# A hybrid block in float32: its gates in blocks of 1024 columns, 14 of 48 groups of eight products as seven, heads from the value projections on, x loaded a second time

## The chip, the cores and the metric

The kernel runs on one core of one Trainium2 chip. Each engine works through its own queue in order: PE (matmuls, with PEld for its weight loads), DVE (VectorE), ACT (ScalarE), POOL (GpSimd) and SP, which here issues most of the DMAs. Times are device microseconds of one execution. The metric is the median of several runs; a separate, profiled execution gives the trace.

## The reference

One transformer block in float32, 256 tokens, width 2048.

```python
h = rms_norm(x, g_mix)
fq, fk, fv, f_logit, sq, sk, sv, mq, gates = split(h @ w_in)
# six forgetting heads, six stick-breaking heads, four memory heads of 128
g = sigmoid(gates.reshape(b, s, 3, 2048) + b_gate)
merged = g[:, :, 0] * (o_fox @ w_br_fox) + g[:, :, 1] * (o_sb @ w_br_sb) + g[:, :, 2] * (o_mem @ w_br_mem)
x = x + merged @ w_out
u = causal_depthwise_conv(rms_norm(x, g_ffn) @ w_up, conv_w, conv_b)
u_gate, u_val = split(u)
x = x + (silu(u_gate) * u_val) @ w_down
```

The gates are the largest product before the feed-forward part: 256 x 2048 times 2048 x 6144.

## The kernel before, in words

**Products.** Every weight is used as a high part, rounded to the matmul's operand type, and a low part, the rest. A product of a 128 x 128 tile of the left side with 128 x 512 weights is three matmuls into one PSUM bank: high times high, low times high, high times low (`passes`, L153). `product` (L161) walks the 2048 rows of a 512-column stripe of weights in pieces of two k tiles. A piece (`piece`, L140) is a DMA of 512 KB on SP into `raw`, a cast on ACT to `hi` (L146) and a subtraction on DVE to `lo` (L147); four buffers of each are in rotation. For two k tiles, two row tiles t of x and one stripe a piece feeds 12 matmuls.

**Order.** `product` calls `tick()` (L110) after each piece. Generators that were put on a list with `later` move on by one stage at each tick, two of them at a time: this is how the attention heads run between the pieces of a projection. `finish()` runs those that are left. A scheduler may move instructions that aren't held in program order (`pin`, L134, holds them while `pinned[0]` is set; `tc.keep_in_program_order` always does).

**Stages around the change.** Projections for the heads come first: names `f0` to `f4` for the forgetting heads, `s0` to `s4` for the stick-breaking ones, where `s3` and `s4` are the values (L595 to L602). The six stick-breaking heads (`sb_head`, L614) are put on the list behind `s4`; each has a product of scores (tile `z`), three functions on ACT, sums along the keys by matmul (tile `r`), an exponential, and the weighted values. Then for each of four 512-column stripes n: three gates (L664 to L673), each with its own `product`, its bias row `bg`, and a read-out on DVE (L670) that scales by the row's norm and adds the bias, with a sigmoid on ACT; then the three branch products, multiplied by the gates (L680 to L687) and transposed. The output projection adds to `xres`, which has held x since the start (L716), and the sum is stored (`xkeep`, L717).

**Eight and seven.** The down projection at the end works in blocks of 1024 columns. There a group is two k tiles, two row tiles and two stripes: eight products, or seven in a scheme that multiplies sums and differences of tiles (`seven`, L966). Four factors are made from the left side (`forms`, L879), four sums from the weights: `T1` to `T4`. In that stage two of these sums are made ahead and come ready from memory (L980), two are made on the spot (L982, L983). `Y` are four further banks that collect products used in more than one place; `gather` (L1014) adds them where they belong.

Of the kernel before, what the change touches and what calls it, by code (L numbers as in the profile page):

```python
# [37 lines left out]
PLANS = ("eeeee" + "se" * 5 + "sse" + "s" + "eee", "e" + "se" * 3 + "sse" * 4 + "see")  # L38
AHEAD = 2
NSEVEN = tuple(plan.count("s") for plan in PLANS)  # L40


@with_exitstack
def hybrid_block(
# [83 lines left out]
    def finish():  # L128
        while waiting or active:
            tick()  # L130
# [458 lines left out]
    for c in range(3):  # L589
# [4 lines left out]
        later(heads_T(y, qs[c], gs, 0, f"s{c}"))  # L594
    ps = proj(C_SB + 1536, 512, "s3")  # L595
    vs[0] = rows_of(block("vs0"))
    for t in range(NT):
        nc.scalar.activation(vs[0][:, t], ps[t], AF.Copy, scale=rstd[:, t : t + 1])
    ps = proj(C_SB + 2048, 256, "s4")
    vs[1] = rows_of(block("vs1"))  # L600
    for t in range(NT):
        nc.scalar.activation(vs[1][:, t, :256], ps[t][:, :256], AF.Copy, scale=rstd[:, t : t + 1])  # L602

    W3 = 3 * P
# [9 lines left out]
    def sb_head(h):  # L614
# [21 lines left out]
        diagonal(lb)  # L636
        yield 2
        weighted(lb, vs, h, N_FOX + h, Z)

    for h in range(N_SB):  # L640
        later(sb_head(h))


# [16 lines left out]

    for n in range(4):
        n0 = n * 512
        gate = []
        for b in range(3):  # L664
            bg = gp.tile([P, 512], F32, tag="bg", name=f"bg_{n}_{b}")
            tc.keep_in_program_order(nc.sync.dma_start(bg, b_gate[0, b, n0 : n0 + 512].partition_broadcast(P)))
            ps = proj(C_GATE + b * D + n0, 512, f"g{n}_{b}")
            g = rows_of(block(f"g_{n}_{b}"))
            for t in range(NT):
                nc.vector.scalar_tensor_tensor(g[:, t], ps[t], rstd[:, t : t + 1], bg, ALU.mult, ALU.add)  # L670
            if n > 0:
                nc.scalar.activation(g, g, AF.Sigmoid)
            gate.append(g)  # L673
        if n == 0:
            finish()
            for g in gate:
                nc.scalar.activation(g, g, AF.Sigmoid)
        acc = rows_of(block(f"acc_{n}"))
        for i, (w, k0, nk, b) in enumerate(branches):
            ps = product(lambda k: oT[:, k0 + k], w[0], nk, n0, 512, f"b{n}_{b}")  # L680
            for t in range(NT):
                g = gate[b]
                if i == 0:
                    nc.vector.tensor_tensor(acc[:, t], g[:, t], ps[t], ALU.mult)
                else:
                    nc.vector.tensor_tensor(g[:, t], g[:, t], ps[t], ALU.mult)
                    nc.vector.tensor_tensor(acc[:, t], acc[:, t], g[:, t], ALU.add)  # L687
        later(merged_T(acc, n))
# [4 lines left out]
    rbc = cst.tile([P, S], F32, name="rbc")  # L693

# [43 lines left out]
    def conv_pool():  # L738
        assert not waiting and not active
        xrs.close()  # L740
# [395 lines left out]
```

## Time and profile before

| | |
|---|---|
| median of 3 runs | 1488.44 us (1487.39 to 1489.52) |
| the profiled execution | 1488.21 us |
| its span, first to last instruction | 1486.5 us |
| PE busy | 1479.5 us, 7408 matmuls |
| DVE busy | 1047.6 us |
| ACT busy | 860.4 us |
| gates (group g of PE, lines L157 to L159) | 3 x 384 = 1152 matmuls of 128 x 512 |
| PE clock granted | 1.000 |

A row of a group names line, engine, operation, out <- in, shapes, count, busy time, mean duration in ns, idle time of the engine just before and what ended it. A matmul's end is modelled, so durations on PE overlap; the distance of starts is the pace. A window's row gives start and end, its length, then busy time and instructions of PE, PEld, DVE, ACT and POOL, the clock, the DMA share and GB/s. A row of waits gives who waited for whom, the total, how often, and the longest.

### The profile page before, as it was taken

The page shows a single profiled execution, that of the slowest core. Times are in us where ns is not written, and L with a number is a line of the kernel's source. Part 1 is how long each engine was busy: PE and PEld are TensorE (multiplying, and loading weights), DVE is VectorE, ACT ScalarE, POOL GpSimd, SP SyncE. Part 2 cuts the span into 40 slices and gives each one's busy share as a digit, 9 for nine tenths or more (in the row PEclk, how much of TensorE's full clock was granted, in tenths as well). Part 3 has the DMA queues.
Part 4 walks back from the last instruction along what each step waited for, and adds up shares of the span by engine and source line. Part 5 has one row for each costly group of instructions (what it writes and reads, how often), then busy time and mean ns, then how long its engine had stood idle before and what let it go on. Part 6 is the DMA issues. An engine that isn't in the chain of part 4 may idle for free.

```text
span 1486.5 us, 20239 instructions
## 1 busy us (share of the span) xinstructions
PE 1479.5 (100%) x7408; PEld 1248.4 (84%) x7408; DVE 1047.6 (70%) x1353; ACT 860.4 (58%) x1231; POOL 40.9 (3%) x91
## 2 busy tenths in 40 slices
PE   9999999999999999999999999999999999999998
PEld 7888888888888888888888888888888888888887
DVE  5767566554655656556556877877877886999997
ACT  6755454358544444444456776776676676665664
POOL 1000000001000000000000000000000000000000
PEclk9999999999999999999999999999999999999999
DMA  8675475475676666656677778778778787777874
GB/s 294 190 203 156 128 223 160 121 228 155 187 203 204 192 203 202 201 187 208 199 222 223 236 268 269 239 267 281 231 274 274 236 275 235 247 252 267 282 284 170
DMA packets 156804, 329.80 MB, mean 222 GB/s; under 512 B 11456, under 2 KB 19952, under 8 KB 156704
## 3 DMA queue, kind: packets, MB, share of 16 engines
q1 hardware_dynamic: 151216, 311.52, 66.6%
q0 software_dynamic: 4736, 15.93, 2.9%
q8 instruction: 58, 0.95, 0.3%
q10 hardware_dynamic: 752, 1.06, 0.2%
q14 instruction: 42, 0.34, 0.1%
HBM read 313.78 MB, written 14.68 MB: 221 GB/s over the span
## 4 chain that ended last, share of the span: by engine, by line
PE 96%; ACT 1%; DVE 1%; DMA 1%; issue 1%; POOL 0%; SPq 0%; DVEq 0%; POOLq 0%; ACTq 0%
PE u L838 22%; PE u L840 11%; PE g L157 5%; PE g L159 5%; PE g L158 5%; PE d L926 5%; PE d L927 5%; PE d L925 5%; PE s L157 2%; PE s L159 2%; PE f L157 2%; PE f L159 2%; PE f L158 2%; PE s L158 2%; PE b L157 2%; PE b L159 2%
## 5 line engine op out<-in xcount | busy, mean ns | idle before, releaser
L838 PE MATMUL u<-hT,hi_u 128*128 128x512 f32 x1408 | 442.4, 396 | 0.1
L840 PEld LDWEIGHTS u<-hT,lo_u 128*128 128x128 f32 x1408 | 264.4, 188 | 62.6 <-DVE lo_u L147 0.2
L840 PE MATMUL u<-hT,lo_u 128*128 128x256 f32 x1408 | 276.7, 278 | 0.0
L147 DVE TENSOR_TENSOR lo_u<-raw_u,hi_u 128x1024 fp32r<-128x1024 f32 x176 | 211.9, 1220 | 81.1 <-ACT hi_u L146 78.8
L146 ACT CAST hi_u<-raw_u 128x1024 fp32r<-128x1024 f32 x176 | 180.5, 1048 | 116.3 <-DMA raw_u<-in_w_up_dram 70.3
L838 PEld LDWEIGHTS u<-hT,hi_u 128*128 128x128 f32 x1408 | 214.3, 189 | 0.5 <-issue 0.5
L147 DVE TENSOR_TENSOR lo_g<-raw_g,hi_g 128x1024 fp32r<-128x1024 f32 x96 | 117.7, 1228 | 101.2 <-ACT hi_g L146 98.5
L146 ACT CAST hi_g<-raw_g 128x1024 fp32r<-128x1024 f32 x96 | 100.8, 1052 | 121.8 <-PE g L158 98.6
L157 PE MATMUL g<-hi_g,xT 128*128 128x512 f32 x384 | 150.9, 393 | 0.0
L159 PE MATMUL g<-lo_g,xT 128*128 128x512 f32 x384 | 149.6, 390 | 0.0
L158 PE MATMUL g<-hi_g,xT 128*128 128x512 f32 x384 | 149.5, 389 | 0.0
L159 PEld LDWEIGHTS g<-lo_g,xT 128*128 128x128 f32 x384 | 72.1, 188 | 15.3
L158 PEld LDWEIGHTS g<-hi_g,xT 128*128 128x128 f32 x384 | 72.1, 188 | 14.6
L157 PEld LDWEIGHTS g<-hi_g,xT 128*128 128x128 f32 x384 | 72.1, 188 | 14.5
L768 ACT ACTIVATE z<-u,taps 128x256 f32<-128x256 f32 x176 | 74.8, 496 | 0.0
L925 PE MATMUL d<-hi_d,aT 128*128 128x512 f32 x192 | 74.7, 389 | 0.0
L926 PE MATMUL d<-hi_d,aT 128*128 128x512 f32 x192 | 74.7, 389 | 0.0
L927 PE MATMUL d<-lo_d,aT 128*128 128x512 f32 x192 | 74.7, 389 | 0.0
L769 DVE TENSOR_TENSOR y<-y,z 128x512 f32<-128x512 f32 x88 | 60.7, 690 | 19.9 <-ACT z L768 16.4
L147 DVE TENSOR_TENSOR lo_s<-raw_s,hi_s 128x1024 fp32r<-128x1024 f32 (+1 forms) x40 | 44.7, 1118 | 37.2 <-ACT hi_s L146 37.0
L147 DVE TENSOR_TENSOR lo_f<-raw_f,hi_f 128x1024 fp32r<-128x1024 f32 (+1 forms) x40 | 44.7, 1119 | 34.5 <-ACT hi_f L146 33.0
L146 ACT CAST hi_f<-raw_f 128x1024 fp32r<-128x1024 f32 (+1 forms) x40 | 38.6, 967 | 52.5 <-PE f L158 47.6
(333 smaller groups left out, 2817.5 us busy)
## 6 DMA issues: line engine op xcount, KB each, us to landing
raw_u<-in_w_up_dram SPq DMA_DIRECT2D x176, 512.0 KB, 4.7
raw_g<-in_w_in_dram SPq DMA_DIRECT2D x96, 512.0 KB, 3.7
raw_d<-in_w_down_dram SPq DMA_DIRECT2D x48, 512.0 KB, 5.2
r<-in_w_down_dram SPq DMA_DIRECT2D x80, 256.0 KB, 6.5
raw_s<-in_w_down_dram SPq DMA_DIRECT2D x40, 512.0 KB, 5.3
raw_f<-in_w_in_dram SPq DMA_DIRECT2D x32, 512.0 KB, 3.7
raw_s<-in_w_in_dram SPq DMA_DIRECT2D x32, 512.0 KB, 3.6
raw_o<-in_w_out_dram SPq DMA_DIRECT2D x32, 512.0 KB, 4.3
```

Source lines behind the costliest of these rows:

```text
L146: pin(nc.scalar.copy(hi[:, :m], raw[:, :m]))
L147: pin(nc.vector.tensor_tensor(lo[:, :m], raw[:, :m], hi[:, :m].bitcast(F32), ALU.subtract))
L157: nc.tensor.matmul(o, lhsT=xh, rhs=wh, start=first, stop=False)
L158: nc.tensor.matmul(o, lhsT=xl, rhs=wh, start=False, stop=False)
L159: nc.tensor.matmul(o, lhsT=xh, rhs=wl, start=False, stop=last)
L768: nc.scalar.activation(z[:, i], u[:, i, j : j + S], AF.Copy, scale=taps_of(j, i))
L769: nc.vector.tensor_tensor(y, y, z, ALU.add)
L838: nc.tensor.matmul(ps, lhsT=hi[:, j, c], rhs=hT[:, k + j, :], start=first, stop=False)
L840: nc.tensor.matmul(ps[:, :S], lhsT=lo[:, j, c], rhs=hT[:, k + j, :S], start=False, stop=last)
L925: nc.tensor.matmul(o, lhsT=ah, rhs=w[0], start=first, stop=False)
L926: nc.tensor.matmul(o, lhsT=al, rhs=w[0], start=False, stop=False)
L927: nc.tensor.matmul(o, lhsT=ah, rhs=w[1], start=False, stop=last)
```

## The change

The gates are computed in two rounds (nn) of three blocks (b), each of 1024 columns and 2048 rows, in steps. A letter of a plan is a group of two k tiles: `e` has eight products in two steps, `s` seven in four steps. Each step has a preparation (load, cast, subtraction) and a use (matmuls); the preparation runs two steps ahead (`AHEAD`). The sums of weights are made in place over the two loaded pieces, by four adds of 512 columns on DVE. The factors made from x (`xf`) serve all blocks; three pairs of k tiles have them. A block's four banks X are read out after the first step of the block that follows, where the read-out isn't `alone`; the four banks Y by `gather` in three ticks behind the last seven. From the second block of the first round on, casts, subtractions and read-outs are held in program order (`first_pin`), until the round ends.

The stick-breaking heads are on the list before `s3` and `s4`, and each waits for its values by name (`until`). Room for four more raw buffers comes from `xres`: x is given up after its norm and transposes, and loaded again on POOL's queue (`xagain`) behind the second round of gates.

```diff
+GATE_PLANS = (("e" * 8, "esesesee", "esesesee"), ("eeesesee", "esesesee", "esesesee"))
+GATE_SEVENS = 3
...
-    gp = mix.enter_context(tc.tile_pool(name="gp", bufs=3))
+    gp = mix.enter_context(tc.tile_pool(name="gp", bufs=4))
...
         yield 2
+        yield from until(f"vs{h // 4}")
         weighted(lb, vs, h, N_FOX + h, Z)
 
     for h in range(N_SB):
         later(sb_head(h))
-
+    ps = proj(C_SB + 1536, 512, "s3")
...
+    issued.add("vs1")
...
+    xrs.close()
+    gx = ctx.enter_context(ExitStack())
+    gxp = gx.enter_context(tc.tile_pool(name="gx", bufs=1, side="right", reuse_waits="tile"))
...
+    def x_forms(p):
...
+        tt(d, two, v[:, 0, :, 1].unsqueeze(1).to_broadcast([P, 2, 2, P]), ALU.subtract)
+        tt(g, v[:, :, 0, 0], v[:, :, 1, 0], ALU.add)
+        tt(r[:, :2], d[:, :, 0], d[:, :, 1], ALU.add)
+        nc.vector.scalar_tensor_tensor(r[:, FS2], r[:, FS1], -1.0, g[:, 0], ALU.mult, ALU.subtract)
+        tt(r[:, FS4], r[:, FS2], g[:, 1], ALU.add)
+        yield
+        nc.scalar.copy(xf[p][:, :, 0], r)
+        yield
+        tt(xf[p][:, :, 1], r, xf[p][:, :, 0].bitcast(F32), ALU.subtract)
...
+    def load_1k(src, name):
+        turns[0] += 1
+        if turns[0] % 2 == 0:
+            raw = gxp.tile([P, PIECE], F32, tag="more", bufs=4, name=name)
+        else:
+            raw = wp.tile([P, PIECE], F32, tag="raw", name=name)
+        keep(nc.sync.dma_start(raw, src))
+        return raw
...
+    def by_seven(p, src, X, Y, name, first, last):
+        k0, k1 = 2 * p, 2 * p + 1
+        w, raw = {}, {}
+        add = lambda o, i: keep(nc.vector.tensor_tensor(o, o, i, ALU.add))
+
+        def p0():
+            raw[0] = load_1k(src(k0), f"raw_{name}_{k0}")
+            (w["00"],) = halves(raw[0][:, :512], f"{name}_{k0}")
+
+        def p1():
+            raw[1] = load_1k(src(k1), f"raw_{name}_{k1}")
+            w["10"], w["11"] = halves(raw[1], f"{name}_{k1}")
+            add(raw[0][:, :512], raw[0][:, 512:])
+            add(raw[0][:, 512:], raw[1][:, 512:])
+            add(raw[1][:, 512:], raw[0][:, :512])
+            add(raw[1][:, :512], raw[1][:, 512:])
+
+        def p2():
+            w["T1"], w["T3"] = halves(raw[0], f"{name}_{p}t13")
+
+        def p3():
+            w["T4"], w["T2"] = halves(raw[1], f"{name}_{p}t42")
+
+        def u0():
...
+            triple(Y[0], x_of(k0, 0), w["00"], first, last)
+
+        def u1():
+            triple(X[0], x_of(k1, 0), w["10"])
+            triple(X[1], xf_of(p, FS4), w["11"])
+
+        def u2():
+            triple(Y[2], xf_of(p, FS1), w["T1"], first, last)
+            triple(Y[3], xf_of(p, FS3), w["T3"], first, last)
+
+        def u3():
+            triple(Y[1], xf_of(p, FS2), w["T2"], first, last)
+            triple(X[2], x_of(k1, 1), w["T4"])
...
+        def gather():
+            gs.extend(rows_of(block(f"{name}_{n}")) for n in range(2))
...
+            pin(nc.scalar.copy(e, Y[0]))
+            stt(gs[0][:, 0], Y[0], rs(0), bgs[0], ALU.add)
+            tt(e, e, Y[1])
+            yield
+            tt(f, e, Y[2])
+            tt(e, e, Y[3])
+            stt(gs[1][:, 0], f, nr(0), bgs[1], ALU.add)
+            yield
+            stt(gs[0][:, 1], e, rs(1), bgs[0], ALU.add)
+            tt(e, e, Y[2])
+            stt(gs[1][:, 1], e, nr(1), bgs[1], ALU.add)
+
+        def evict():
...
+            for t in range(NT):
+                for n in range(2):
+                    stt(gs[n][:, t], X[2 * t + n], rs(t), gs[n][:, t] if ns else bgs[n], ALU.add)
...
+        end = len(g_steps) - 1
+        behind(end, finish)
+        behind(end if alone else end + 1, evict)
+        for n in range(2):
+            behind(end if alone else end + 5 + n, lambda n=n: curve(n))
...
+    for nn in range(2):
         for b in range(3):
...
+            gate_block(nn, b, GATE_PLANS[nn][b], b == 2)
...
+        if nn == 1:
+            gx.close()
...
+            for n in range(4):
+                c = slice(n * 512, (n + 1) * 512)
+                nc.gpsimd.dma_start(xres[:, :, c], xv[:, :, c])
```

**PE, the second seven of block b = 1 of the first round.** In a name such as `hi_g_1_3`, 1 is the gate and 3 the k tile; `1t` are sums of the seven with number 1; `g_1_x` and `g_1_y` are banks. Before, where a bank is named by gate and row tile (`g_1_0`), the two row tiles of the same k tile in a piece of 512 columns:

```order
L157 MATMUL g_1_0_3075<-hi_g_1_2_3118,xT 128x512
L158 MATMUL g_1_0_3075<-hi_g_1_2_3118,xT 128x512
L159 MATMUL g_1_0_3075<-lo_g_1_2_3119,xT 128x512
L157 MATMUL g_1_1_3076<-hi_g_1_2_3118,xT 128x512
L158 MATMUL g_1_1_3076<-hi_g_1_2_3118,xT 128x512
L159 MATMUL g_1_1_3076<-lo_g_1_2_3119,xT 128x512
```

and in the change:

```order
L715 MATMUL g_1_y_3417<-hi_g_1_2_3462,xT 128x512
L716 MATMUL g_1_y_3417<-hi_g_1_2_3462,xT 128x512
L717 MATMUL g_1_y_3417<-lo_g_1_2_3463,xT 128x512
L715 MATMUL g_1_x_3365<-hi_g_1_3_3480,xT 128x512
L716 MATMUL g_1_x_3365<-hi_g_1_3_3480,xT 128x512
L717 MATMUL g_1_x_3365<-lo_g_1_3_3481,xT 128x512
L715 MATMUL g_1_x_3366<-hi_g_1_3_3480,xf_2922 128x512
L716 MATMUL g_1_x_3366<-hi_g_1_3_3480,xf_2922 128x512
L717 MATMUL g_1_x_3366<-lo_g_1_3_3481,xf_2922 128x512
L715 MATMUL g_1_y_3419<-hi_g_1_1t_3500,xf_2922 128x512
L716 MATMUL g_1_y_3419<-hi_g_1_1t_3500,xf_2922 128x512
L715 MATMUL g_1_y_3420<-hi_g_1_1t_3500,xf_2922 128x512
```

The same weights now feed banks x and y, with x or a factor of it (`xf`) as the left side; a seven has 21 such rows where two k tiles by two stripes had 24.

**DVE, from the read-out of the first block to the first seven of the second.** Before, at the same gate, subtractions follow each other, with heads between:

```order
L147 TENSOR_TENSOR lo_g_0_8_2976<-raw_g_0_8_2974,hi_g_0_8_2975 128x1024
L626 SCALAR_TENSOR_TENSOR sb_2898<-z_2899,sb_2898 128x384
L627 TENSOR_TENSOR sb_2898<-sb_2898,z_2899 128x384
L626 SCALAR_TENSOR_TENSOR sb_2909<-z_2910,sb_2909 128x384
L627 TENSOR_TENSOR sb_2909<-sb_2909,z_2910 128x384
L147 TENSOR_TENSOR lo_g_0_10_3010<-raw_g_0_10_3008,hi_g_0_10_3009 128x1024
```

and in the change:

```order
L809 SCALAR_TENSOR_TENSOR g_0_0_3381<-g_0_x_2944,rstd,bg_g_0_0_2984 128x512
L809 SCALAR_TENSOR_TENSOR g_0_1_3382<-g_0_x_2945,rstd,bg_g_0_1_2986 128x512
L711 TENSOR_TENSOR lo_g_1_1_3390<-raw_g_1_1_3387,hi_g_1_1_3389 128x1024
L756 TENSOR_TENSOR raw_g_1_0_3359<-raw_g_1_0_3359 128x512
L756 TENSOR_TENSOR raw_g_1_0_3359<-raw_g_1_0_3359,raw_g_1_1_3387 128x512
L756 TENSOR_TENSOR raw_g_1_1_3387<-raw_g_1_1_3387,raw_g_1_0_3359 128x512
L756 TENSOR_TENSOR raw_g_1_1_3387<-raw_g_1_1_3387 128x512
L711 TENSOR_TENSOR lo_g_1_0t_3414<-raw_g_1_0_3359,hi_g_1_0t_3413 128x1024
L711 TENSOR_TENSOR lo_g_1_0t_3425<-raw_g_1_1_3387,hi_g_1_0t_3424 128x1024
```

The read-out (L809) stands ahead of the second load's subtraction, and the four adds (L756) between that and the subtractions of the sums.

**ACT, at the scores of a pair of heads.** `sb` is a head's tile; ACT takes Abs, Exp and Ln of its scores z. Before, at the second pair:

```order
L677 ACTIVATE g_0_3070<-g_0_3070 128x1024
L178 CAST oT<-z_2910 128x256
L146 CAST hi_g_1_8_3172<-raw_g_1_8_3171 128x1024
L623 ACTIVATE sb_3095<-z_3096 128x384
L624 ACT_TABLE_LOAD
L624 ACTIVATE sb_3095<-sb_3095 128x384
L623 ACTIVATE sb_3106<-z_3107 128x384
L625 ACT_TABLE_LOAD
L625 ACTIVATE sb_3095<-sb_3095 128x384
```

and in the change:

```order
L710 CAST hi_g_0_11_3030<-raw_g_0_11_3028 128x1024
L616 ACTIVATE sb_2988<-z_2989 128x384
L617 ACTIVATE sb_2988<-sb_2988 128x384
L616 ACTIVATE sb_2999<-z_3000 128x384
L618 ACTIVATE sb_2988<-sb_2988 128x384
L617 ACTIVATE sb_2999<-sb_2999 128x384
L618 ACTIVATE sb_2999<-sb_2999 128x384
```

The gate's sigmoid (L677) no longer comes before a pair, and no table load stands within one. The order of ACT holds 17 table loads before and 5 in the change.

More of the change, by code (lines that the diff above doesn't have):

```diff
@@ L594, in hybrid_block @@
         later(heads_T(y, qs[c], gs, 0, f"s{c}"))
[L595 to L602, printed above, removed]
     W3 = 3 * P
@@ L641, in hybrid_block @@
         later(sb_head(h))
+    ps = proj(C_SB + 1536, 512, "s3")
+    vs[0] = rows_of(block("vs0"))
+    for t in range(NT):
+        nc.scalar.activation(vs[0][:, t], ps[t], AF.Copy, scale=rstd[:, t : t + 1])
+    ps = proj(C_SB + 2048, 256, "s4")
+    issued.add("vs0")
+    vs[1] = rows_of(block("vs1"))
+    for t in range(NT):
+        nc.scalar.activation(vs[1][:, t, :256], ps[t][:, :256], AF.Copy, scale=rstd[:, t : t + 1])
+    issued.add("vs1")
     mT = [None] * (KT // 2)
@@ L659, in merged_T @@
             yield
-    for n in range(4):
-        n0 = n * 512
-        gate = []
-        for b in range(3):
[L665 to L688, printed above, removed]
```

134 lines of the change are left out of this document (132 added, 2 removed).

## The prediction

> **What bounds the kernel now.** I read the page's first part, then the waits of PE, then PE's timeline in the gate stage.
>
> ```profile
> span 1486.5 us, 20239 instructions
> PE 1479.5 (100%) x7408; PEld 1248.4 (84%) x7408; DVE 1047.6 (70%) x1353; ACT 860.4 (58%) x1231; POOL 40.9 (3%) x91
> ```
>
> ```profile
> PE spare L101 <- DVE qscale L251: 1.2, 1, 1.2
> PE kv L159 <- DVE lo_kv L147: 0.5, 1, 0.5
> PE d L926 <- DVE aT L901: 0.3, 1, 0.3
> PE mT L186 <- DMA memres<-in_mem_dram: 0.2, 1, 0.2
> ```
>
> PE is busy for all but 7 us of the span, and no row of its waits lies in the gate stage. So PE's instructions set the end there, and the question is what one of them is worth. The timeline of PE in the gates (start, duration) shows it:
>
> ```profile
> 439.98 0.39 PE L158 MATMUL g<-hi_g,xT 128*128 128x512 f32 x1
> ...
> 474.89 0.39 PE L159 MATMUL g<-lo_g,xT 128*128 128x512 f32 x1
> ```
>
> Between these two stand 154 starts (155 rows, no other PE work): 34.91 / 154 = 0.2267 us from start to start. The 0.39 us that a row shows as its duration runs on under the next one. A matmul taken away is worth 0.227 us, not 0.39; with 0.39 the same sum comes out 1.7 times too large.
>
> **Matmuls removed.** A group of eight products is 8 x 3 = 24 matmuls, 5.44 us; one of seven is 21, 4.76 us. The order of PE has 42 rows fewer, 14 x 3, and after the gates the same rows as before. 42 x 0.2267 = 9.5 us leave the engine that sets the end.
>
> The Trainium skill ("TensorE: Matmul & The Clock Gate", Back-to-back issue gap) gives a stream of loads of weights and matmuls of 512 columns about 131 ns each, and about 216 ns where matmuls stand alone; by these the sum would be, as estimates, 5.5 or 9.1 us. The stream in these rows has a weight load for each matmul and takes 227 ns, so the measurement decides.
>
> **What the sevens ask of DVE and ACT.** The pieces' casts and subtractions, the gates' read-out, the down stage's sums of two halves (the nearest rows for the adds over the loads) and DVE's timeline there:
>
> ```profile
> L147 DVE TENSOR_TENSOR lo_g<-raw_g,hi_g 128x1024 fp32r<-128x1024 f32 x96 | 117.7, 1228 | 101.2 <-ACT hi_g L146 98.5 <-PE r L633 1.5
> L146 ACT CAST hi_g<-raw_g 128x1024 fp32r<-128x1024 f32 x96 | 100.8, 1052 | 121.8 <-PE g L158 98.6 <-PE b L158 20.0 <-DMA raw_g<-in_w_in_dram 1.6
> L670 DVE SCALAR_TENSOR_TENSOR g<-g,rstd,bg 128x512 f32<-128x512 f32 x24 | 17.4, 748 | 0.0
> ```
>
> ```profile
> L921 DVE TENSOR_TENSOR lo_s<-raw_s,hi_s 128x512 fp32r<-128x512 f32 x20 | 13.7, 685 | 0.5 <-ACT hi_s L920 0.5
> L982 DVE TENSOR_TENSOR t<-raw_s 128x512 f32<-128x512 f32 x20 | 13.7, 684 | 0.0
> L983 DVE TENSOR_TENSOR t<-raw_s,raw_s 128x512 f32<-128x512 f32 x20 | 13.7, 684 | 0.0
> ```
>
> ```profile
> 1364.87 0.69 DVE L1028 TENSOR_TENSOR xr<-xr,e 128x512 f32<-128x512 f32 x1
> 1365.59 0.69 DVE L1029 TENSOR_TENSOR e<-e,d 128x512 f32<-128x512 f32 x1
> ...
> 1382.97 1.22 DVE L921 TENSOR_TENSOR lo_s<-raw_s,hi_s 128x1024 fp32r<-128x1024 f32 x1
> 1384.10 0.68 DVE L982 TENSOR_TENSOR t<-raw_s 128x512 f32<-128x512 f32 x1
> 1384.71 0.68 DVE L983 TENSOR_TENSOR t<-raw_s,raw_s 128x512 f32<-128x512 f32 x1
> ```
>
> From start to start a 1024-wide subtraction takes 1.13 us, a half 0.61, and one that reads what the one ahead wrote 0.72. A seven has a half subtraction, three whole ones and four adds, one of which depends on its neighbour: 0.6 + 3.4 + 2.5 = 6.5 us, against 4.76 us of PE. An eight has two subtractions, 2.26 us, against 5.44. A block with three sevens and five eights also reads out eight banks in twelve operations of about 0.7 us, 8.4. That makes 19.5 + 11.3 + 8.4 = 39.2 us of DVE beside 3 x 4.76 + 5 x 5.44 = 41.5 us of PE, 94%. By whole durations it is 3 x 7.1 + 5 x 2.45 + 8 x 0.748 + 4 x 0.684 = 42.3 us, 102%. I take the former, since it is how these rows stand in time, and because the down stage has run so:
>
> ```profile
> 1366.00:1482.00 116.00, 116.00 (x513) 95.87 (x511) 106.61 (x139) 65.36 (x76) 4.34 (x8) 1.00 0.71 249
> 408.00:475.00 67.00, 67.00 (x301) 55.45 (x300) 36.78 (x38) 28.68 (x30) 0.00 (x0) 1.00 0.68 202
> ```
>
> The windows (PE, PEld, DVE, ACT, POOL) give the down stage's second half, with twelve sevens: DVE busy 106.6 of 116 us, 92%, PE 116 of 116. The gates of before (second row) use 55% of DVE. So the gates become what the down stage is already.
>
> The share hides the order, so I walk one "seven, eight" period on the four hi/lo buffers, PE's start of the seven at 0, with a cast 1.05. PE takes the seven's four steps until 0.68, 2.04, 3.40, 4.76, the eight's two until 7.48 and 10.20. A buffer comes free four steps on, so the next seven's casts may start at 3.4, 4.8, 7.5 and 10.2. Its first subtraction ends at 4.8, the second (cast until 5.9) at 7.1, its adds run to 9.6, two of them done at 8.3. The cast of the first pair of sums ends at 9.4, its subtraction at 10.7; the second pair's cast at 11.3, subtraction at 12.4. PE wants them at 12.2 and 13.6. The following eight's cast and subtraction end at 12.4 and 13.5, wanted at 15.0. Slack is 1.2 us or more everywhere: no cost in the steady state, bounds 0 and what the third rival gives.
>
> At a boundary the read-out comes on top. Walked the same way from a block with sevens into the next one, DVE does the gather and two subtractions until 14.9 us after the last seven's start, waits 0.8 for a buffer that PE holds to the block's end, then evicts (2.8) ahead of the next seven's second subtraction; its first sums are ready within 0.3 us of when PE wants them, before or after. Three boundaries are of this kind: 1.0 us, bounds 0 and 5 (the second rival).
>
> The factors made from x are 18 DVE operations of 128 to 512 columns, some 8 us, three casts, in the first block, where eight eights take 18 of 43.5 us of DVE and four heads some 8: hidden. Without that cover they would cost their 8 us once.
>
> **Heads.** Their instructions are the same; they move ahead of two value projections. In the order of ACT the sigmoids no longer stand between heads, and table loads fall from 17 to 5. Before, in the groups of ACT and PE of the stretch that holds the last heads:
>
> ```profile
> L624 ACT ACT_TABLE_LOAD x4 | 5.1, 1283 | 0.1
> L625 ACT ACT_TABLE_LOAD x4 | 5.1, 1283 | 0.1
> L677 ACT ACT_TABLE_LOAD x3 | 3.8, 1283 | 0.1
> L635 ACT ACT_TABLE_LOAD x2 | 2.6, 1283 | 0.0
> L632 PE MATMUL r<-sb,ones 128*128 128x128 f32 x8 | 1.7, 300 | 0.3
> ```
>
> PE waited 0.3 us for a head's sums, behind loads that now go: -0.3. Against it, the steps of the 256-column projection are short, so the first pair has less cover. PE would wait there if the chain still held three or four of those loads, 4 to 5 us once. I take nothing, since the order has none there.
>
> **Loads.** A piece of gate weights is still 512 KB, and eight raw buffers stand in for four.
>
> ```profile
> SPq L145 <- DVE lo_g L147: 204.4, 88, 6.8
> raw_g<-in_w_in_dram SPq DMA_DIRECT2D x96, 512.0 KB, 3.7
> T<-r POOLq DMA_DIRECT2D x20, 512.0 KB, 8.8
> ```
>
> SP's queue waits for buffers, not for landings (204 us in the gates); ACT's row above waited 1.6 us for gate data in 96 casts. 1 MB in 4.76 us is 220 GB/s, under the 249 of the down window. The four reloads of x go out on POOL's queue, which holds nothing else until x is stored; at 8.8 us each, one after another, they take 35 us, and x is first wanted after two branch rounds and one output round, 3 x 96 x 0.2267 = 65 us. Hidden by these; if not, 35 us at most.
>
> **Sum.** The profiled execution took 1488.21 us, 1.7 of them outside the span, and stands 0.2 under the median of the runs. 1488.2 - 9.5 - 0.3 + 1.0 = 1479.4, or 1479.6 beside the median.
>
> **Rivals.**
>
> PE's count decides, as above: 1479.6, chance 0.72.
>
> DVE becomes the bound in the four blocks with three sevens. If its operations take their whole durations, each block is 0.8 us longer than PE's, 3.2, and the boundaries 1.0 to 2.0 more: 5 us, which gives 1483.6. For it: 94 to 102% by the two counts. Against it: the down window. Chance 0.13.
> The Trainium skill ("VectorE: DVE Perf Modes", The DRAIN you can't avoid) says that the next operation starts only when the pipe is empty, with operations that are not held as the exception; by the first half this rival would be the rule. The starts 0.61 us apart of operations of 0.68 are the exception.
>
> The sums' chain sets the pace (the other side). Unlike in the down stage, no part of the sums comes ready from memory: both pairs wait for adds on the two loads. If cast, subtraction, adds and the casts of the sums ran end to end, with the eight's two subtractions ahead, it would be 2.45 + 1.05 + 1.22 + 2.74 + 2 x (1.05 + 1.22) = 12.0 us from the buffer's release at 4.8 to 16.8, where PE wants its eight at 15.0. That is 1.8 us in each of 14 sevens, 25 us: 1503.6. It decides from 0.7 us a seven, where the 9.5 are used up. For it: in-order queues, and ACT behind PE in 98.6 us of waits. Against it: two or more of these run beside each other in the walk. Chance 0.07.
>
> Heads wait in the short projection: 4 us, 1483.6. Chance 0.05. That the matmuls stay is excluded by the order. Mixtures of small waits, 5 to 8 us, hold the last 0.03.
>
> **Numbers.** The low end is the sum without any wait, 1478.6, less 1 us of spread of the runs: 1477.5. The high end takes in the second and fourth case with the same spread: 1485.0. About 0.2%, 3 us, is what a measurement of this kernel can tell from no change. Faster by more: 0.72 + 0.11 + 0.03 = 0.86, since parts of the second and fourth case lie nearer. Slower: 0.07. Within: 0.07.
>
> **What would show it.** In the changed profile: gate matmuls (group g of PE) 1110 instead of 1152 and still 0.227 us apart; PE's waits in the gates under 2 us in all; DVE near 94% in blocks with three sevens; one table load for the sigmoids; x landed well before the first output tile is added. Wrong it is if PE waits for hi or lo of the sums in most sevens (third rival), or if PE's starts stretch over whole blocks while DVE never idles (second).

## The result and the profile after

The changed kernel took 1480.16 us (median of 4 runs, 1478.54 to 1481.43) beside 1488.30 for the kernel before: a ratio of 0.9944, 95% interval 0.9927 to 0.9961. A second set, the same kernel timed among the experiments, gave 1479.75 (5 runs) and 0.9950, 0.9937 to 0.9962. Forecast were 1479.6.

The page of the profiled execution, which took 1481.43 us and was the slowest of its four:

```profile
span 1479.7 us, 20357 instructions
PE 1471.5 (99%) x7366; PEld 1239.8 (84%) x7366; DVE 1134.7 (77%) x1496; ACT 866.9 (59%) x1255; POOL 42.3 (3%) x95
```

42 matmuls fewer (7366 against 7408), and 143 DVE instructions more. PE's timeline tells where the stages begin; first before, then after (start, duration; group `s` are the projections of the stick-breaking heads, `u` the up-projection, `d` the down projection):

```profile
193.61 0.40 PE L157 MATMUL s<-hi_s,xT 128*128 128x512 f32 x1
...
763.99 0.47 PE L838 MATMUL u<-hT,hi_u 128*128 128x512 f32 x1
```

```profile
194.04 0.40 PE L159 MATMUL s<-hi_s,xT 128*128 128x512 f32 x1
...
755.30 0.47 PE L1059 MATMUL u<-hT,hi_u 128*128 128x512 f32 x1
...
1248.76 0.40 PE L1146 MATMUL d<-hi_d,aT 128*128 128x512 f32 x1
```

From `s` to `u` it was 570.38 us and is 561.26: 9.1 us won. Everything that was changed lies between these two. The up-projection behind it, whose code is the same, took 493.46 us here, and 491.68 before: 1.8 us were lost again in this one execution. The table below gives both lengths for each kernel that was run, since the time alone mixes them. (The expectations call the first of them "from the first short projection to the up-projection".)

**PE's pace.** In the second round of gates PE never stops. The first and last of 485 rows in a row that hold one matmul each, all of the gates:

```profile
509.87 0.39 PE L716 MATMUL g_x<-hi_g,xT 128*128 128x512 f32 x1
...
619.59 0.39 PE L717 MATMUL g_x<-lo_g,xT 128*128 128x512 f32 x1
```

109.72 / 484 = 0.2267 us, as before, through two blocks and a half with eight sevens. The first round has seven clearly longer distances of starts: four in the second seven of the second block (1.06 us in excess of the pace), one in the first seven of the third block (0.10) and two in its second seven (0.27). With the small ones, the 366 gate matmuls of these two blocks take 84.45 us from the first start to the last, 1.6 us more than in the kernel without adds below (82.87), which has no long step. The first place:

```profile
382.21 0.39 PE L717 MATMUL g_x<-lo_g,xf 128*128 128x512 f32 x1
382.87 0.50 PE L715 MATMUL g_y<-hi_g_1t,xf 128*128 128x512 f32 x1 [0.26 <-ACT hi_g_1t L710]
...
383.67 0.40 PE L716 MATMUL g_y<-hi_g_1t,xf 128*128 128x512 f32 x1
384.31 0.50 PE L715 MATMUL g_y<-hi_g_1t,xf 128*128 128x512 f32 x1 [0.25 <-ACT hi_g_1t L710]
```

Mind the brackets: they say 0.26 and 0.25 us, since a row's idle time is counted from the modelled end of the matmul ahead. Against the pace of 0.227 the two steps lost 0.43 and 0.41, and the matmul behind each another 0.1. PE waits for the cast of the sums `hi_g_1t`. ACT's timeline shows why it is late:

```profile
373.36 1.28 ACT L844 ACT_TABLE_LOAD   x1
374.65 1.06 ACT L844 ACTIVATE g<-g 128x1024 f32<-128x1024 f32 x1
375.62 1.03 ACT L710 CAST hi_g<-raw_g 128x1024 fp32r<-128x1024 f32 x1
376.56 1.05 ACT L844 ACTIVATE g<-g 128x1024 f32<-128x1024 f32 x1
377.51 1.55 ACT L710 CAST hi_g<-raw_g 128x512 fp32r<-128x512 f32 x2
381.76 1.05 ACT L710 CAST hi_g_1t<-raw_g 128x1024 fp32r<-128x1024 f32 x1 [2.70 <-DVE raw_g L756]
```

The table load and two sigmoids of the block that was just read out, 3.4 us, stand ahead of the casts of the second seven's pieces (377.51); DVE's subtractions and adds follow those, and the cast of the sums waits for the adds (L756).

### The profile page after: what moved, and what is told of

Its sections match the earlier page's. It is cut to its first block, busy times and chain, and to the rows that moved or that the text cites. A ratio compares the mean times of both kernels' runs of the same rounds, so it can differ in the third digit from the quotient of the medians.

```text
span 1479.7 us, 20357 instructions
## 1 busy us (share of the span) xinstructions
PE 1471.5 (99%) x7366; PEld 1239.8 (84%) x7366; DVE 1134.7 (77%) x1496; ACT 866.9 (59%) x1255; POOL 42.3 (3%) x95
## 3 DMA queue, kind: packets, MB, share of 16 engines
q10 hardware_dynamic: 752, 1.06, 0.2%
## 4 chain that ended last, share of the span: by engine, by line
PE 94%; DMA 2%; DVE 2%; ACT 1%; issue 1%; SPq 0%; DVEq 0%; ACTq 0%
PE u L1059 20%; PE u L1061 10%; PE d L1147 5%; PE d L1148 5%; PE d L1146 5%; PE g_x L715 5%; PE g_x L717 5%; PE g_x L716 5%; PE s L159 2%; PE s L161 2%; PE f L161 2%; PE f L159 2%; PE f L160 2%; PE s L160 2%; PE b L161 2%; PE b L159 2%
## 5 line engine op out<-in xcount | busy, mean ns | idle before, releaser
L711 DVE TENSOR_TENSOR lo_g<-raw_g,hi_g 128x1024 fp32r<-128x1024 f32 (+1 forms) x96 | 108.1, 1143 | 34.1 <-ACT hi_g L710 31.7
L710 ACT CAST hi_g<-raw_g 128x1024 fp32r<-128x1024 f32 (+1 forms) x96 | 92.6, 985 | 60.7 <-PE g_x L716 50.4
L715 PE MATMUL g_x<-hi_g,xT 128*128 128x512 f32 x286 | 112.2, 392 | 0.0
L717 PE MATMUL g_x<-lo_g,xT 128*128 128x512 f32 x286 | 111.4, 390 | 0.0
L716 PE MATMUL g_x<-hi_g,xT 128*128 128x512 f32 x286 | 111.3, 389 | 0.0
L149 DVE TENSOR_TENSOR lo_o<-raw_o,hi_o 128x1024 fp32r<-128x1024 f32 x32 | 39.2, 1225 | 35.4 <-ACT hi_o L148 30.9
L148 ACT CAST hi_s<-raw_s 128x1024 fp32r<-128x1024 f32 (+1 forms) x40 | 38.4, 960 | 42.8 <-PE s L160 35.4
L717 PEld LDWEIGHTS g_x<-lo_g,xT 128*128 128x128 f32 x286 | 53.7, 188 | 11.5
```

Of the source, the lines that this page charges most:

```text
L148: pin(nc.scalar.copy(hi[:, :m], raw[:, :m]))
L149: pin(nc.vector.tensor_tensor(lo[:, :m], raw[:, :m], hi[:, :m].bitcast(F32), ALU.subtract))
L710: pin(nc.scalar.copy(hi[:, :n], src))
L711: pin(nc.vector.tensor_tensor(lo[:, :n], src, hi[:, :n].bitcast(F32), ALU.subtract))
L715: nc.tensor.matmul(o, lhsT=a[0], rhs=w[0], start=first, stop=False)
L716: nc.tensor.matmul(o, lhsT=a[1], rhs=w[0], start=False, stop=False)
```

## What the experiments were to tell apart

The theory after the first trace: PE's count makes the gain, the sigmoids cost 1.3 us of it. Rivals: the gain comes from the other parts of the change (blocks, order, heads); DVE has no room left; the sevens slow the up-projection. From the traces, in us (the gaps are what all steps between matmuls of the gates took over PE's pace in the last two blocks of the first round and in the second round, less the 0.1 us that an unbroken stretch of them has in every kernel; the expectations count the long steps alone, 1.3 us in the change):

| kernel | `s` to `u` | gaps | up-projection | median |
|---|---|---|---|---|
| before | 570.38 | 0 | 491.68 | 1488.30 |
| the change | 561.26 | 1.6 | 493.46 | 1480.16 |
| the change again | 561.29 | 1.6 | 496.72 | 1479.75 |
| no sevens | 569.20 | 0 | 491.64 | 1486.84 |
| late sigmoids | 560.73 | 1.1 | 492.74 | 1480.09 |
| split sigmoids, early table | 564.38 | 4.5 | 493.29 | 1481.52 |
| no adds | 559.67 | 0 | 496.68 | 1482.07 |
| late sigmoids, read-out in halves | 559.83 | 0.2 | 496.71 | 1482.57 |
| the same and a 15th seven | 559.75 | 0.6 | 492.43 | 1477.63 |
| two more adds | 565.47 | 5.0 | 491.55 | 1485.19 |
| four sevens a block | 572.05 | 15.4 | 492.64 | 1492.08 |
| heads behind the values | 570.15 | 3.5 | 493.35 | 1488.76 |
| four raw buffers | 582.89 | 23.4 | 491.56 | 1498.00 |
| no rows beside the up-projection | 561.24 | 1.6 | 491.66 | 1479.60 |

## The sevens against the rest of the change

```diff
-GATE_PLANS = (("e" * 8, "esesesee", "esesesee"), ("eeesesee", "esesesee", "esesesee"))
-GATE_SEVENS = 3
+GATE_PLANS = (("e" * 8,) * 3,) * 2
+GATE_SEVENS = 0
```

> Every group of the gates is an eight; blocks of 1024 columns, the moved heads, eight raw buffers and the second load of x stay. Theory (PE's count decides, less about 1.3 us of waits behind the sigmoids in the second sevens of two blocks): 42 matmuls come back, 42 x 0.2267 = 9.5 us, and the waits go with the sevens: 1480.2 + 9.5 - 1.3 = 1488.4, between 1487.3 and 1489.0, and no gap in PE's pace in the gates. Rival (blocks, order and heads bring a good part of the gain): 1484 or less.

1486.84 us, a ratio of 0.9990 (0.9981 to 0.9998) to the kernel before, and no gap in the gates. That is under the expected range by 0.5 us. The sevens are worth 569.20 - 561.26 = 7.9 us in the traces, which is 9.5 less the gaps of 1.6; the rest of the change is worth 570.38 - 569.20 = 1.2, not the 0.3 that were forecast. (Beside the kernel without adds, below, which has the sevens and no gap, it is 569.20 - 559.67 = 9.53 us, where 42 x 0.2267 is 9.52.) Half of the 1.2 is PE's wait for a head's sums in the kernel before, which stands there twice:

```profile
349.55 0.60 PE L631 MATMUL r<-sb,after 128*128 128x256 f32 x2
350.30 0.49 PE L632 MATMUL r<-sb,ones 128*128 128x128 f32 x2
...
376.24 0.60 PE L631 MATMUL r<-sb,after 128*128 128x256 f32 x2
376.98 0.49 PE L632 MATMUL r<-sb,ones 128*128 128x128 f32 x2
```

The second of each pair starts 0.75 and 0.74 us behind the first; without sevens, in the moved heads, it is 0.43:

```profile
302.70 0.59 PE L624 MATMUL r<-sb,after 128*128 128x256 f32 x2
303.13 0.38 PE L625 MATMUL r<-sb,ones 128*128 128x128 f32 x2
```

So 0.63 us, of which the idle column showed 0.3. The other 0.6 us has no single place in the trace.

## Where the heads stand

```diff
-    for h in range(N_SB):
-        later(sb_head(h))
     ps = proj(C_SB + 1536, 512, "s3")
...
     issued.add("vs1")
+    for h in range(N_SB):
+        later(sb_head(h))
```

> Only the moved heads are undone: they are put on the list behind the second value projection, as in the kernel before. Theory: 16 steps of the first block don't hold three pairs, and the last pair drains at the block's end with nothing beside it on PE: from scores to sums abs, exp, ln, two of DVE and the select, about 4 to 5 us with table loads, and from sums to values add, exp and select, about 3 us: 1480.2 + 8, between 1486 and 1491. Rival (the place of the heads is worth only the 0.3 us that was predicted): 1480.5.

1488.76 us, within the theory's range: `s` to `u` is 8.9 us longer. PE's timeline at the end of the first block, with the last pair alone:

```profile
361.22 0.38 PE L615 MATMUL z<-qk_sb,qk_sb 128*128 128x128 f32 x2
365.33 1.22 PE L624 MATMUL r<-sb,after 128*128 128x256 f32 x2 [3.73 <-POOL sb L602]
```

PE waits 3.7 us for POOL's selection, and then runs slowly (1.22 us for two matmuls that took 0.59 above); of that below. The theory's second wait, 3 us from the sums to the values, does not show: about as much is lost to the slow stretch, and some 2 us to longer waits in the sevens behind. The place of the heads is thus no part of the gain by itself, but a condition of it: blocks of 1024 columns leave 16 steps for three pairs, where the kernel before had 24 in its first three gates. The change would have won next to nothing without it.

## The sigmoids and the boundary

```diff
-            behind(end if alone else end + 5 + n, lambda n=n: curve(n))
+            behind(end if alone else end + 17 + 2 * n, lambda n=n: curve(n))
```

> The two sigmoids of a block that is read out in the next one are issued behind that block's steps 17 and 19 (in its last eights) instead of 5 and 6. Theory (the casts of the second seven's sums stand behind these sigmoids and their table load on ACT): the gaps of about 1.05 us at PE's second seven of block 1 and 0.26 us of block 2 of the first round go, 1480.2 - 1.3 = 1478.9, and no new gap comes. Rival (the gaps are DVE's read-out and adds, which have no room): the gaps stay, 1480.2.

The gaps of the second sevens are gone, and one that wasn't there appears at the first seven of the third block:

```profile
413.44 0.39 PE L717 MATMUL g_x<-lo_g,xf 128*128 128x512 f32 x1
413.96 0.50 PE L715 MATMUL g_y<-hi_g_0t,xf 128*128 128x512 f32 x1
```

0.94 us in all there, so only 0.5 us is won from `s` to `u`, too little for the time to show (1480.09). No sigmoid stands ahead of that seven on ACT. DVE's timeline does not pause (no bracket in these rows):

```profile
404.70 2.96 DVE L711 TENSOR_TENSOR lo_g<-raw_g,hi_g 128x1024 fp32r<-128x1024 f32 x3
407.57 2.72 DVE L809 SCALAR_TENSOR_TENSOR g<-g_x,rstd,g 128x512 f32<-128x512 f32 x4
410.21 1.21 DVE L711 TENSOR_TENSOR lo_g<-raw_g,hi_g 128x1024 fp32r<-128x1024 f32 x1
411.34 0.68 DVE L756 TENSOR_TENSOR raw_g<-raw_g 128x512 f32<-128x512 f32 x1
```

The four operations of the read-out (L809) stand ahead of the last subtraction and the adds (L756). This is the wait that the prediction worked out for the boundaries. In the change only the 0.10 us at that place are left of it, since PE, held up by 1.06 us in the block ahead, comes later: the two waits take each other's place and do not add.

A second attempt put the sigmoids one by one into eights, and the table load ahead of the block:

```diff
-            behind(end if alone else end + 5 + n, lambda n=n: curve(n))
+            behind(end if alone else end + 11 + 6 * n, lambda n=n: curve(n))
...
         pinned[0] = True
+        seen = oT[:, N_FOX + N_SB - 1, :NT].bitcast(F32)
+        pin(nc.scalar.activation(warm, seen, AF.Sigmoid))
```

> The table of the sigmoid is loaded at the end of the first block, behind the last head, by a sigmoid of two columns that nothing reads; the two sigmoids of a block stand behind steps 11 and 17 of the next one, one in each of two eights, instead of 5 and 6. Theory (two sigmoids and a table load in one place, 3.4 us on ACT, are what the casts of sums can't take; 1.05 us can be taken): no gap is left in the gates, from the first short projection to the up-projection 560.0 us instead of 561.3, and 1478.9 in all. Rival (any sigmoid in front of a seven costs its time): gaps elsewhere, as when both were moved to the block's end, 560.7 us, no change of the time.

Both were wrong: 564.38, 3.1 us longer than the change. The load had to wait for the last head, and the casts of the block's first seven are held behind it in ACT's order:

```profile
365.52 1.28 ACT L881 ACT_TABLE_LOAD   x1
...
366.93 1.55 ACT L710 CAST hi_g<-raw_g 128x512 fp32r<-128x512 f32 x2
373.44 1.04 ACT L710 CAST hi_g_0t<-raw_g 128x1024 fp32r<-128x1024 f32 x1 [4.96 <-DVE raw_g L756]
```

In the change these two casts ran at 362.67, ahead of the last head's; here they come some 4 us later, and the sums with them. The gap at that seven is the only long one left in the gates, so the places behind steps 11 and 17 do no harm themselves.

Then the read-out was halved, with the sigmoids late:

```diff
-            for t in range(NT):
-                for n in range(2):
-                    stt(gs[n][:, t], X[2 * t + n], rs(t), gs[n][:, t] if ns else bgs[n], ALU.add)
+            for n in range(2):
+                stt(gs[n][:, 0], X[n], rs(0), gs[n][:, 0] if ns else bgs[n], ALU.add)
...
+        def evict2():
+            for n in range(2):
+                stt(gs[n][:, 1], X[2 + n], rs(1), gs[n][:, 1] if ns else bgs[n], ALU.add)
...
+        behind(end if alone else end + 2, evict2)
```

> The late sigmoids (behind steps 17 and 19), and the read-out of a block in halves: two banks where all four were read, two a step later, behind the adds of the first seven. Theory (with the sigmoids gone from there, DVE's read-out ahead of the adds at the block's boundary sets the wait, 0.9 us at the first seven of the third block): the adds come 1.4 us earlier there, no gap is left, 559.8 to 560.0 us from the first short projection to the up-projection instead of 560.7. Rival (DVE works without a pause there, so what comes earlier for the first seven comes later for the second): a gap of 0.5 us or more elsewhere in that block, 560.5 or more. In the median 1479.3 against 1480.1, too near to tell.

559.83 us and no long step in the gates, as the theory had it. DVE works without a pause here too, but in another order:

```profile
406.70 1.40 DVE L809 SCALAR_TENSOR_TENSOR g<-g_x,rstd,g 128x512 f32<-128x512 f32 x2
408.02 1.22 DVE L711 TENSOR_TENSOR lo_g<-raw_g,hi_g 128x1024 fp32r<-128x1024 f32 x1
409.15 0.69 DVE L756 TENSOR_TENSOR raw_g<-raw_g 128x512 f32<-128x512 f32 x1
...
411.93 1.40 DVE L809 SCALAR_TENSOR_TENSOR g<-g_x,rstd,g 128x512 f32<-128x512 f32 x2
```

The median, 1482.57 (1478.04 to 1484.65), is longer than that of the change all the same. The trace shows where: the up-projection took 496.71 us.

## How near DVE is to its limit

Four runs change how much DVE has to do, two of them with the number of sevens. First without the adds:

```diff
-            add(raw[0][:, :512], raw[0][:, 512:])
-            add(raw[0][:, 512:], raw[1][:, 512:])
-            add(raw[1][:, 512:], raw[0][:, :512])
-            add(raw[1][:, :512], raw[1][:, 512:])
```

> The four adds over the loads are left out, so the sums T1 to T4 are the loaded pieces themselves: the sevens' products, and with them the gates, aren't the reference's. Theory (PE's count decides; the only price of the sums is the 1.3 us of waits in the second sevens): these waits go, 1480.2 - 1.3 = 1478.9, and from the first short projection to the up-projection the trace shows 560.0 us instead of 561.3. Rival (DVE's load costs time in other places too, which no wait of PE shows): 1477.5 or less.

559.67 us where the theory had 560.0, since it counted the long steps alone; so 1.6 us is all that the adds cost, and the late sigmoids with the halved read-out get it back but for 0.2. The median, 1482.07, again has an up-projection of 496.68 in it.

Then two more, and then a fourth seven:

```diff
+            for c in "ab":
+                z = sm.tile([P, 512], F32, tag="junk", bufs=2, name=f"z{c}_{name}_{p}")
+                keep(nc.vector.tensor_tensor(z, raw[0][:, :512], raw[0][:, 512:], ALU.add))
```

> Each seven gets two more adds of 128x512 on DVE into a scratch tile that nothing reads. Theory (DVE, at 39.5 to 40.4 us in blocks of 41.8, has about 1.5 us left): two times 0.61 in each of three sevens is 3.7 us a block, so 43.2 to 44.1 against 41.5: 1.7 to 2.6 us in each of four blocks, some 7 to 10 us in all, 1487 to 1490. Rival (what DVE idles can be filled, and only chains of waits count): 1480 to 1482.

```diff
-GATE_PLANS = (("e" * 8, "esesesee", "esesesee"), ("eeesesee", "esesesee", "esesesee"))
-GATE_SEVENS = 3
+GATE_PLANS = (("e" * 8, "essesese", "essesese"), ("eeesesee", "essesese", "essesese"))
+GATE_SEVENS = 4
```

> The four blocks with three sevens get four; a fourth pair of factors of x is made in the first block. PE has 12 matmuls fewer than with three, 2.7 us. Theory (DVE is near its ceiling): by the distances of starts a block asks DVE for 4 x 6.5 + 4 x 2.26 + 8.4 = 43.4 us against 40.8 of PE, so DVE sets the pace of these blocks: 43.4 - 41.5 = 1.9 us more than now in each, 1487.8, or 1488 to 1491 with the 39.5 to 40.4 us that DVE shows now and 4.1 for one seven in place of an eight. Rival (the casts behind the sigmoids were the only limit): 1480.2 - 2.7 = 1477.5.

1485.19 and 1492.08 us. The windows of the two last blocks of each round (start and end, length, then busy time of PE, PEld, DVE), of the change, of two more adds and of four sevens:

```profile
364.50:449.20 84.70, 84.19 (x369) 68.50 (x368) 79.88 (x95) 46.91 (x52) 0.00 (x0) 1.00 0.53 173
536.00:619.80 83.80, 83.80 (x371) 69.39 (x370) 80.08 (x95) 48.01 (x51) 2.86 (x4) 1.00 0.60 195
```

```profile
363.00:449.40 86.40, 84.73 (x368) 67.74 (x367) 84.19 (x104) 46.73 (x52) 0.00 (x0) 1.00 0.49 165
535.00:621.50 86.50, 85.85 (x377) 69.93 (x376) 85.89 (x106) 47.09 (x51) 2.86 (x4) 1.00 0.56 187
```

```profile
365.10:457.20 92.10, 85.94 (x364) 68.09 (x363) 86.06 (x103) 50.76 (x56) 0.00 (x0) 0.98 0.49 160
544.00:631.40 87.40, 84.19 (x365) 67.75 (x364) 85.56 (x103) 50.35 (x55) 2.86 (x4) 1.00 0.56 181
```

The change keeps DVE busy for 94 and 96% of these blocks, and PE does not wait in the second. With two more adds it is 97 and 99%, and `s` to `u` 4.2 us longer: less than the 7 to 10 expected, because more of DVE's idle time could be filled than the theory allowed, but the sign is its own. The new long steps stand at the first seven of the third block of either round (1.28 us between starts at 413.06, 0.79 at 585.9). The fourth seven takes 12 matmuls (2.7 us) from PE, and `s` to `u` is 10.8 us longer, so 1492.08 lies above the 1488 to 1491 of the theory. DVE's shares, 93 and 98%, are no higher than with two more adds: DVE does not set the pace by its count alone. PE's long waits are for the casts of the sums in the first seven behind a boundary (up to 1.73 us between starts) and above all in the second, which in this plan follows the first directly (up to 2.15); the last two sevens of a block have none. ACT in turn waits there for DVE's adds. So it is the chain of the sums over DVE and ACT that becomes the bound, one seven a block further on; that two sevens in a row are the reason was not tried by itself.

The last of these adds a third seven where DVE has room, in the first block of the second round, to the kernel with late sigmoids and a halved read-out:

```diff
-("eeesesee", "esesesee", "esesesee"))
+("esesesee", "esesesee", "esesesee"))
```

> As the kernel with late sigmoids and a halved read-out, and a third seven in the first block of the second round, 15 in all. Theory (that block has room on DVE: 35.2 of 42.3 us, and a seven in place of an eight adds 4.2): three matmuls fewer, 0.68 us: 559.2 us from the first short projection to the up-projection, 1478.6. Rival (DVE at 39.4 of 41.6 us pushes the read-out into the next block's first seven): 560.0 or more, no gain.

559.75 us: of the 0.68 us only 0.08 arrived, and three longer steps, 0.36 us over the pace, are new at that block's second seven. The rival's place was wrong, its size nearly right. The median is 1477.63 (1477.13 to 1478.61), 0.9929 of the kernel before (0.9916 to 0.9943), and the lowest of all. In the traces 1.5 us of its lead over the change are the sigmoids' and the read-out's places and the 15th seven; the rest, 1.0 us, is of the size by which the up-projection differs between executions, and isn't shown to be its own.

## Eight raw buffers, and x a second time

```diff
-        if turns[0] % 2 == 0:
-            raw = gxp.tile([P, PIECE], F32, tag="more", bufs=4, name=name)
-        else:
-            raw = wp.tile([P, PIECE], F32, tag="raw", name=name)
+        raw = wp.tile([P, PIECE], F32, tag="raw", name=name)
...
-    xrs.close()
...
-                nc.gpsimd.dma_start(xres[:, :, c], xv[:, :, c])
```

> x stays where it was and isn't loaded again, so the gates have four raw buffers as before, not eight; the sevens stay. Theory (the room that x gives is what makes the sevens free): a seven's two buffers are held until its sums are subtracted, at 10.7 and 12.4 us of the walk, and a load of 4.7 us then ends at 15.4 and 17.1, where the seven behind wants its casts at 13.6 and 15.0; 2 us late with 1.2 us of slack is about 0.9 us in each of some eight periods: 1480.2 + 7, between 1483 and 1495. Rival (the loads are hidden with four as well, and the reload of x only costs): 1480 or less.

1498.00 us, slower than the kernel before. The theory's sign holds, its 7 us were too few: `s` to `u` is 21.6 us longer. ACT now waits for data in the gates, where the change has a wait of 1.7 us in the groups of its casts:

```profile
ACT hi_g L704 <- DMA raw_g<-in_w_in_dram: 35.5, 25, 2.6
PE g_y L709 <- ACT hi_g_2t L704: 6.6, 8, 1.3
PE g_y L709 <- ACT hi_g_1t L704: 5.3, 8, 1.2
```

So the room that x gave up carries the sevens. No price of it shows: the reload leaves at 613 us, the first row of x is added 73 us later, and PE has no wait for it.

```profile
613.19 2.86 POOL L896 DMA_DIRECT2D xagain<-in_x_dram  x4 [252.38 <-DVE lo_g L711]
...
686.55 1.37 DVE L937 TENSOR_TENSOR xagain<-xagain,o 128x512 f32<-128x512 f32 x2
```

## What is lost behind the gates

> The changed kernel itself, unaltered. Theory (what the first trace lost behind the gates, 1.9 us in the up-projection, is a matter of when its loads land in one execution, not of the change's order): the gates show the same gaps, 1.3 us, and the same 561.3 us from the first short projection to the up-projection within 0.3; the up-projection, 493.5 us in the first trace and 491.6 to 496.7 in the others, has another length. Rival (the sevens shift the up-projection for good): 493.5 again within 0.2. The median stays at 1480.2 within 1.0.

The same kernel, not edited: the same gaps at the same places, 561.29 us, and an up-projection of 496.72, not 493.46. The rival is out: its length belongs to the execution. (This profiled execution took 1484.38 us, the slowest of its five.) What moves is when its loads land. Waits of ACT in that stretch, of the kernel before, of the change, and of the change again (total, number, longest):

```profile
ACT hi_u L146 <- DMA raw_u<-in_w_up_dram: 70.3, 24, 4.5
```

```profile
ACT hi_u L148 <- DMA raw_u<-in_w_up_dram: 105.5, 38, 4.9
```

```profile
ACT hi_u L148 <- DMA raw_u<-in_w_up_dram: 125.9, 44, 5.5
```

Beside these loads run the rows of the down projection's weights, 80 loads of 256 KB, for the sums that are made ahead. They were taken out:

```diff
-        for j, n in ((0, 1), (0, 0), (1, 1), (1, 0)):
-            tc.keep_in_program_order(
-                nc.sync.dma_start(r[j][:, n], dv[:, 2 * p + j, n0 + n * 512 : n0 + (n + 1) * 512])
-            )
-            yield 1
+        r = [zeros[0], zeros[1 + len(made) % 2]]
+        for _ in range(4):
+            yield 1
```

> The changed kernel, but the rows of the down projection's weights that are loaded beside the up-projection for the sums made ahead (20 times 1 MB) are left out; zeros stand in their place, so the output isn't the reference's. The gates are as in the change. Theory (the up-projection's length differs from execution to execution because its own loads land late beside these): 561.3 us from the first short projection to the up-projection with gaps of 1.3, the up-projection 491.6 within 0.3 instead of 493.5 and 496.7, and runs closer together, all between 1478.3 and 1480.8. Rival (the loss there isn't a matter of loads): 493 or more, and runs up to 1482 or more.

The up-projection took 491.66 us, the runs lie between 1478.34 and 1479.79, and ACT waits for PE, no longer for data:

```profile
ACT hi_u L148 <- PE u L1060: 95.1, 65, 2.1
```

So the up-projection is close to what its loads allow, and 0 to 5 us are lost there from one execution to the next. ACT's waits for data don't give that loss by themselves: in the trace with the halved read-out they are 86.8 us, with the 15th seven 98.3, and the up-projection is 496.71 and 492.43. What goes with it is how far they reach PE: its weight loads wait for DVE's low parts of `u` for 7.3 us in the change again, 2.7 in the change, 0.9 with the 15th seven and 0.2 in the kernel before. That the runs without the rows lie close together proves little alone, since those with the 15th seven do so too, with these loads in place (1477.13 to 1478.61). What stays open: the kernel before issues the same loads, and all its runs lie between 1487.15 and 1489.59, while seven of the kernels made here spread over 4 us or more. Why some kernels lose there more often than others wasn't found.

## Why the prediction held, and where it didn't

**Matmuls removed, 42 x 0.2267 = 9.5 us.** Right: the pace held through the whole second round, and taking the sevens out again costs 7.9 us in the traces, just this sum less the gaps of 1.6. The gates hold 1110 matmuls, and their sigmoids one table load, the one at 373.36.

**What the sevens ask of DVE: nothing in the steady state.** Right, and the count by starts was the one to take: 94 and 96% of the windows, where whole durations gave 102%. One reading in it was off: three of the four adds, not one, stand 0.72 us apart (starts 380.24, 380.96 and 382.41 in the first round), so a seven's adds take 2.8 us, not 2.5, and a block some 0.8 us more than was counted. The walk of one period with 1.2 us of slack agrees with 485 matmuls in a row.

**Boundaries, 1.0 us.** Near in size (1.6 by all steps) by luck, wrong in its reason as it stood. The walk over the boundary left out the table load and the two sigmoids, 3.4 us on ACT, which the change issues five and six steps into the next block. Their wait in the second sevens came first, and hid the wait of the read-out that had been worked out; with the sigmoids gone from there it stood where it was forecast, 0.94 us, at one of the three boundaries. The two others, in the second round, cost nothing in the change.

**Heads, 0.3 us.** Mis-sized: all that isn't sevens brought 1.2 us. The wait was read off the idle column, which is counted from a matmul's modelled end; the distances of starts show 0.63 for it. The wait that the fourth rival had in the short projection did not come: no row of PE's waits lies there.

**Loads and the reload of x, nothing.** Right: 73 us of room for four loads. The price without this cover was given as 35 us for the reload only; that without the eight buffers is what counts, and it is 18 us in the median (the run without them also leaves out the reload).

**The sum, 1479.6.** 1480.16 and 1479.75 were measured. From `s` to `u` 9.1 us were won where 8.8 were forecast; the difference to the median is of the size of the up-projection's, a term that the sum did not have, and the smaller errors of the other terms, 0.6 us too little for the boundaries and 0.9 for the heads, nearly cancel. Without the rows beside the up-projection the median is 1479.60, 9.1 us under the 1488.68 of the kernel before in the same set.

**The rivals.** That DVE becomes the bound (1483.6) did not happen with three sevens; the prediction's 94% named the margin, but not how few operations it holds: two adds a seven are more than it. The sums' chain as the pace (1503.6) is excluded by the second round for this kernel. PE does wait for that chain with four sevens a block, and with four raw buffers, there behind loads that come late, which this rival did not have.

## What to carry to other kernels

Price a matmul, and a wait of PE, by the distance of starts, never by the duration or the idle column of its row. When an engine is at 95% of the pace, write out its whole order over a block's boundary, with what another engine puts in front of the same chain, and expect waits to change places rather than to add. An edit that saves work on one engine often stands on others that make room for it: each of them is tested by undoing it alone.

## What the runs showed of the hardware

A short wait of PE can cost more than itself. In the kernel with the early table load PE waited 1.73 us once at 372.8. The window ahead of the slow stretch, and that stretch itself (length, PE, PEld, DVE, ACT, POOL, then the granted clock):

```profile
372.84:376.25 3.41, 1.45 (x5) 0.94 (x6) 3.31 (x5) 2.40 (x3) 0.00 (x0) 1.00 0.00 0
376.25:379.66 3.41, 3.41 (x9) 2.62 (x9) 3.41 (x4) 3.00 (x4) 0.00 (x0) 0.50 0.75 205
```

From 376.25 to 379.66 the clock is 0.50, and matmuls start 0.43 us apart: about 1.7 us lost on top of the wait. With the heads behind the values the wait of 3.73 us was followed by 6.8 us at 0.50. The two waits of 0.4 us in the change had no such end. The kernel with four sevens has both cases in one trace:

```profile
376.81:380.22 3.41, 1.91 (x6) 0.95 (x6) 3.31 (x5) 1.68 (x2) 0.00 (x0) 1.00 0.21 83
424.59:428.00 3.41, 1.40 (x6) 0.85 (x6) 3.29 (x5) 2.32 (x3) 0.00 (x0) 1.00 0.11 46
428.01:431.42 3.41, 3.41 (x9) 2.64 (x9) 3.41 (x4) 2.95 (x4) 0.00 (x0) 0.50 0.74 199
```

The first of these windows was laid 14 lengths of 3.41 us ahead of the second; PE was busy for 1.91 us of it, and the clock stayed at 1.00. With four raw buffers two slow stretches, 47.79 us or 14 such lengths apart, follow windows with 1.79 and 1.78 us of busy PE. So in these traces the bound lies between 1.79 and 1.91 us of 3.41, if the windows do lie on a fixed grid, which the distance of 14 lengths suggests but doesn't prove. The Trainium skill ("TensorE: Matmul & The Clock Gate", Part 1) has the clock halved after an idle window of about 3.4 us. The half clock itself and its length agree; here a window in which PE was busy for 1.79 of 3.41 us was enough.
